# A decoder layer on one core: one gate pair moved from plain products in attention to the seven-product form

## The chip, the cores and the metric

The kernel runs on one core of a Trainium2 chip. The metric is the time of one execution in device microseconds; a time given for a kernel is the median of several runs. A profiled execution, taken by the hardware profiler, gives the rows that are read below. Engines: PE is TensorE's matrix products (PEld its weight loads), DVE is VectorE, ACT is ScalarE, POOL is GpSimd, SP is SyncE, which issues most of the loads.

## What is computed

One layer of a decoder on 512 tokens of width 1024, in float32. The parts around the change, shortened:

```python
proj = h @ w_in[l]
q, k, v, p, g = jnp.split(proj, [ATTN_WIDTH, 2 * ATTN_WIDTH, 3 * ATTN_WIDTH, 3 * ATTN_WIDTH + POOL_WIDTH], axis=-1)
y_attn = moba_attention(q.reshape(hs), k.reshape(hs), v.reshape(hs), rel_bias) @ w_branch_attn[l]
y_pool = multiscale_pool(p, w_pool_group[l], pool_scale[l]) @ w_branch_pool[l]
gates = jax.nn.sigmoid(g.astype(jnp.float32)).astype(h.dtype).reshape(B, S, N_BRANCHES, D)
mixed = gates[:, :, 0] * y_attn + gates[:, :, 1] * y_pool
h = layer_norm(ALPHA * h + mixed @ w_out[l], ln1_g[l], ln1_b[l])
a, u = jnp.split(h @ w_ffn_in[l], 2, axis=-1)
a = causal_dwconv(a, conv_w[l], conv_b[l])
f = (jax.nn.gelu(a, approximate=False) * u) @ w_ffn_out[l]
h = layer_norm(ALPHA * h + f, ln2_g[l], ln2_b[l])
```

Attention has 8 heads of 64. The gates are 2 x 1024 columns of the input projection: 8 output tiles of 128 for the attention branch and 8 for the pooling branch. A tile f of the first and the tile f of the second make a gate pair.

## The kernel before

**Products.** Every float32 operand is split into hi and lo parts (`split`, L71 to L78: ACT copies hi, DVE subtracts to get lo). `mm3` (L241) makes a product of three: hi by hi (L243), hi weight by lo activation (L246), lo weight by hi activation (L247). A plain output tile (`in_tile`, L491) takes 8 row blocks x 3 products of 512 columns, 24 in all. A branch tile (`br_mm`, L640) has 4 row blocks: 12 products of 512.

**The seven-product form.** `seven` (L285) computes two output tiles at once as a 2 x 2 block product with seven block products in place of eight. The tokens are halved (t1, t2 of 256), the rows of the weights too. It needs four combinations of the activations, called nT1, T3, nT2, T4, formed once by `t_form` (L261; subtractions at L264 and L267) and split; and combinations of the two weight tiles: A is the first tile as loaded, X a sum that the DMA makes (a plain load on SP at L188, an accumulating one on POOL at L190), D half of the second tile, Y comes from A and X by two DVE additions (L207). Each of the seven takes 4 row blocks x 3 products of 256 columns.

**Order of the stages.** v, the pooling tiles and q, k come first. Then attention runs as a loop over heads h = 0 to 7 (L656), two heads ahead: `head(h + 2)` casts keys and queries (k, kl the low part of the keys, q) and copies k and kl to the other 64 partitions by DMA (L454); then one filler for PE; `scores(h + 2)` (products sc; DVE adds the bias from strip and takes maxima nm, ACT takes exponentials at L561, POOL normalises at L566); `pv` of a pair of heads (products ob, L634); `trans(h)` (transposes tr, L621, copied to PT). The fillers of heads 0 to 3 are four plain gate tiles (g0, g8, g1, g9, `fill`); those of heads 4 to 7 are pooling-branch tiles (`early_branch`, L649; names br0_1 to br3_1, the 1 for pooling).

After the loop oT, the attention output (copied at L636), is split into oT_hi and oT_lo, and `order` (L708) lists the other branch tiles: br4_1, br5_1, br6_1, then the attention-branch tiles br6_0, br0_0 to br5_0. Beside them the four forms of x for the gates are made from four quads, which POOL loads at L676 behind the last normalisation, followed by X of the first gate pair (gX). Then six gate pairs f = 2 to 7 follow in the seven-product form (products sag, scg, sbg), then the tile br7 of both branches, the output projection (wo), and the FFN.

**What sets the order.** Each engine works through its own queue in the order in which a scheduler has put the instructions; `issue_after` forbids some to be put earlier. A PE product whose input is late keeps everything behind it waiting.

Of the kernel before, what the change touches and what calls it, by code (L numbers as in the profile page):

```python
# [8 lines left out]
F32 = mybir.dt.float32  # L9
# [5 lines left out]
P = 128  # L15
S = 512
# [3 lines left out]
H = 8  # L20
# [18 lines left out]
RAW = 1  # L39
KH = NF // 2  # L40
TAIL = 8
GSEVEN = 2
BRANCH = (("z", 0), ("z", 1), ("z", 2), ("br", 6), ("o", 0), ("o", 1), ("o", 2), ("br", 7))
SEVEN = tuple(range(2, 19))
COVER = 4
# [7 lines left out]
def layer_kernel(ctx: ExitStack, tc: tile.TileContext, xT, x, w_v, w_c, rel_bias, invcnt, w_group,  # L53
# [18 lines left out]
    def split(hi, lo, src, copy=None):  # L72
        if copy:
            copy(hi, src)
        else:
            state["hi"] = nc.scalar.activation(hi, src, AF.Copy)  # L76
        state["lo"] = nc.vector.tensor_tensor(lo, src, hi.bitcast(F32), op=ALU.subtract)  # L77
        return state["lo"]  # L78
# [8 lines left out]
    def add(key, *tiles):  # L87
        at[key] = len(chunks)
        chunks.extend(tiles)

    def add_seven(key, *two):
        pair_of[key] = two
        for q in "AXDY":
            add((*key, q), (key, q))
# [4 lines left out]
    for p in range(pairs):  # L99
        add_seven(("i", 1 + p), w_c[first["q"] + p], w_c[first["k"] + p])  # L100
    fill = [("g", 8 * g + f) for f in range(GSEVEN) for g in range(2)]
    for n, j in fill:
        add((n, j), w_c[first[n] + j])
    for n, key in enumerate(BRANCH[:-1]):
        add(key, w_br[n])
    for f in range(GSEVEN, KT):
        add_seven(("g", f), w_c[first["g"] + f], w_c[first["g"] + KT + f])
# [208 lines left out]
    zT = keepp.enter_context(tc.tile_pool(name="keepz", bufs=1)).tile([P, 4, S], F32, name="zT")  # L316
# [120 lines left out]
    def head(h, *behind):  # L437
        p, e = divmod(h, 2)
        own, oth = slice(e * DH, (e + 1) * DH), slice((1 - e) * DH, (2 - e) * DH)
        qb, kb = raw_q[p], raw_k[p]  # L440
        Q1[h] = av.tile([P, S], F32R, tag="q1", name=f"q1_{h}")
        K1[h] = av.tile([P, S], F32R, tag="k1", name=f"k1_{h}")
        KL[h] = av.tile([P, S], F32R, tag="kl", name=f"kl_{h}")
        with ExitStack() as held:
            for ins in behind:
                held.enter_context(tc.issue_after(ins.ins))
            nc.scalar.activation(K1[h][own, :], kb[own, :], AF.Copy, scale=-1.0)
            nc.vector.scalar_tensor_tensor(KL[h][own, :], kb[own, :], -1.0, K1[h][own, :].bitcast(F32),
                                           op0=ALU.mult, op1=ALU.subtract)
            nc.scalar.activation(flip(Q1[h][own, :]), qb[own, :], AF.Copy, scale=DH ** -0.5)  # L450
            nc.vector.scalar_tensor_tensor(flip(Q1[h][oth, :]), qb[own, :], DH ** -0.5,
                                           flip(Q1[h][own, :]).bitcast(F32), op0=ALU.mult, op1=ALU.subtract)
        for t in (K1[h], KL[h]):
            state["dup"] = nc.sync.dma_start(t[oth, :].bitcast(F32), t[own, :].bitcast(F32))  # L454
# [36 lines left out]
    def in_tile(kind, j):  # L491
        wh, wl = split3(weights(at[kind, j]), KT)
        b = bank(f"{kind}{j}")
        for kt in range(KT):
            mm3(b, (wh[:, kt, :], wl[:, kt, :]), (xT_hi[:, kt, :], xT_lo[:, kt, :]), kt == 0, kt == KT - 1)
        if kind == "p":
            return b
        else:
            gslot[j] = gates[:, len(gslot), :]
            nc.scalar.activation(gslot[j], b, AF.Copy)  # L500
# [39 lines left out]
    def scores(h):  # L540
        if h + 2 < H:
            load_strip(h + 2)
        pp = aw.tile([P, 10 * P], F32, tag="pp", name=f"pp{h}")
        nm = aw.tile([P, NT], F32, tag="nm", name=f"nm{h}")
        rs = aw.tile([P, NT], F32, tag="rs", name=f"rs{h}")
        b01 = bank(f"sc{h}_01")
        dst = [b01[:, :2 * P], b01[:, 2 * P:], bank(f"sc{h}_2")[:, :3 * P], bank(f"sc{h}_3")]
        for i in range(NT):
            n = max(2, i + 1) * P
            q = slice(i * P, (i + 1) * P)  # L550
            nc.tensor.matmul(dst[i], Q1[h][:, q], K1[h][:, :n], start=True, stop=False)
            nc.tensor.matmul(dst[i], Q1[h][:, q], KL[h][:, :n], start=False, stop=True)
        for i in range(NT):
            n = (i + 1) * P
            nc.vector.tensor_tensor_reduce(out=pp[:, offs[i]:offs[i] + n], in0=dst[i][:, :n],
                                           in1=strips[h][:, S - n:], scale=1.0, scalar=-3.0e38,
                                           op0=ALU.add, op1=ALU.max, accum_out=nm[:, i:i + 1])
        nms[h] = nc.vector.tensor_scalar(nm, nm, -1.0, None, op0=ALU.mult)  # L558
        for i in range(NT):
            n = (i + 1) * P  # L560
            exps[h] = nc.scalar.activation(pp[:, offs[i]:offs[i] + n], pp[:, offs[i]:offs[i] + n], AF.Exp,  # L561
                                           bias=nm[:, i:i + 1], accum_out=rs[:, i:i + 1])
        nc.vector.reciprocal(rs, rs)  # L563
        for i in range(NT):
            n = (i + 1) * P
            state["norm"] = nc.gpsimd.tensor_scalar(pp[:, offs[i]:offs[i] + n], pp[:, offs[i]:offs[i] + n], rs[:, i:i + 1], 1.0,  # L566
                                    op0=ALU.mult, op1=ALU.mult)
        Ps[h] = pp
# [33 lines left out]
            scores(0)  # L602
    phase.close()
    keep = keepp.enter_context(tc.tile_pool(name="keep", bufs=1, reuse_waits="tile"))
    gates = keep.tile([P, 2 * GSEVEN + 4, S], F32, name="gates")
    oT = keep.tile([P, 4, S], F32, name="oT")
    zT_hi = keep.tile([P, 4, S], F32R, name="zT_hi")
    zT_lo = keep.tile([P, 4, S], F32R, name="zT_lo")
# [31 lines left out]
    def br_mm(f, br, b=None, ks=range(4), pin=False):  # L640
        key, o = (("br", f), 4 * br) if f >= 6 else (("oz"[br], f // 2), f % 2 * 4)
        wh, wl = split3(weights(at[key]), KT)
        b = b or bank(f"br{f}_{br}")
        for k in ks:
            src = (zT_hi[:, k, :], zT_lo[:, k, :]) if br else (oT_hi[:, k, :], oT_lo[:, k, :])
            mm3(b, (wh[:, o + k, :], wl[:, o + k, :]), src, k == 0, k == 3, pin and k == ks[0])
        return b

    def early_branch(f):  # L649
        t = branch[f, 1] = gates[:, 2 * GSEVEN + f, :]  # L650
        nc.vector.tensor_copy(t, br_mm(f, 1))
# [4 lines left out]
    for h in range(H):  # L656
        if h + 2 < H:
            head(h + 2, nms[h], exps[h])
        if h < 4:
            in_tile(*fill.pop(0))  # L660
        elif h < H - 1:
            early_branch(h - 4)
        if h + 2 < H:
            scores(h + 2)
        with ExitStack() as held:
            if h and h % 2 == 0:
                pv(h // 2 - 1)
                held.enter_context(tc.issue_after(state["pv"].ins))
            trans(h)
        if h < 4:  # L670
            with tc.issue_after(nms[h].ins), tc.issue_after(exps[h].ins):
                split(zT_hi[:, h, :], zT_lo[:, h, :], zT[:, h, :])
        if h == 5:
            with tc.issue_after(state["norm"].ins), tc.issue_after(state["dup"].ins):
                for n, (k, t) in enumerate(((k1, t1), (k1, t2), (k2, t1), (k2, t2))):
                    nc.gpsimd.dma_start(quads[n], xT[k.start * P:k.stop * P, t].rearrange("(k p) t -> p k t", p=P))  # L676
                homes["g", "X"], homes["g", "D"] = lambda f: gX, lambda f: gD
                for q in "XD":
                    coming[q].remove(("g", GSEVEN))
                    fetch_raw(("g", GSEVEN), q)  # L680
                    homes.pop(("g", q))
        if h == H - 1:
            early_branch(h - 4)
    pv(H // 2 - 1)
    attn.close()

# [4 lines left out]
    more = bp.tile([P, 4, S], F32, name="more")  # L691
# [11 lines left out]
        nc.gpsimd.tensor_tensor(a, b, a, op=ALU.add)  # L703
        mts[f] = a

    unused = [more[:, n, :] for n in range(4)]
    forms = list(parts)
    order = [(4, 1), (5, 1), (6, 1), (6, 0)] + [(f, 0) for f in range(6)]  # L708
    for n, (f, br) in enumerate(order):
        if f < GSEVEN:  # L710
            with tc.issue_after(state["o"].ins):
# [35 lines left out]
    for f in range(GSEVEN, KT):  # L747
        if f == KT - 1:
# [3 lines left out]
              lambda ba, u, f=f: gate_done(f, ba, u), first_half if f == KT - 1 else None)  # L752
# [434 lines left out]
```

## Time and profile before

| | before |
|---|---|
| median of 3 runs | 627.27 us (626.81 to 627.68) |
| the profiled execution | 627.02 us, span 625.3 us |
| mean granted TensorE clock | 0.995 |
| PE busy | 615.4 us (98%) |
| DVE busy | 514.8 us (82%) |
| ACT busy | 361.6 us (58%) |
| POOL busy | 119.4 us (19%) |

Busy time of PE counts products that overlap as one stretch; the time that a product adds is the distance from its start to the next start. In the rows a timeline line gives start and duration, both in us from the span's start, then engine, line, operation, output and inputs, and in brackets the idle time before it with what ended that.

### The profile page before, as it was taken

What the parts mean: (1) busy time and instruction counts of PE and PEld (TensorE: products, weight loads), DVE (VectorE), ACT (ScalarE), POOL (GpSimd) and SP (SyncE); (2) the same over time, 40 slices, a digit from 0 to 9 for tenths busy, and PEclk for the clock granted to TensorE, in tenths of its full rate; (3) what the DMA queues carried; (4) which work ended last, traced back from release to release, by engine and by line L of the source; (5) the groups of instructions that cost most, each with busy time, mean ns of one, the idle gap of its engine ahead of it and who ended that gap; (6) DMA issues with size and microseconds to landing.
All of it is one profiled execution on the core that took longest, in us unless ns stands there. A gap on an engine that the chain in (4) does not pass through costs nothing.

```text
span 625.3 us, 10604 instructions
## 1 busy us (share of the span) xinstructions
PE 615.4 (98%) x4060; PEld 554.7 (89%) x4060; DVE 514.8 (82%) x790; ACT 361.6 (58%) x552; POOL 119.4 (19%) x133
## 2 busy tenths in 40 slices
PE   8999999999999999999999999999999999999994
PEld 6899998786799998889999999999999888888884
DVE  5978788784967988399989988898988859698886
ACT  5746778663756567125566566566656356555442
POOL 0133135244032101110110101101100302123302
PEclk9999999999999999999999999999999999999998
DMA  8566747435386414806658777678635996899805
GB/s 313 168 191 192 172 122 226 123 118 185 118 206 181 102 67 171 301 36 210 161 167 215 181 197 186 180 195 206 184 96 163 329 248 134 211 194 207 197 0 135
DMA packets 41634, 109.29 MB, mean 175 GB/s; under 512 B 4448, under 2 KB 4712, under 8 KB 41328
## 3 DMA queue, kind: packets, MB, share of 16 engines
q1 hardware_dynamic: 27808, 72.42, 33.9%
q0 software_dynamic: 13200, 35.15, 29.2%
q10 hardware_dynamic: 576, 1.05, 0.5%
q8 instruction: 32, 0.52, 0.3%
q14 instruction: 18, 0.15, 0.1%
HBM read 104.39 MB, written 3.17 MB: 172 GB/s over the span
## 4 chain that ended last, share of the span: by engine, by line
PE 97%; DVE 1%; DMA 1%; ACT 0%; POOL 0%; issue 0%; DVEq 0%; POOLq 0%; ACTq 0%
PE saf L243 5%; PE saf L247 5%; PE saf L246 5%; PE v L426 3%; PE fi L243 3%; PE fi L246 3%; PE fi L247 3%; PE sbf L243 3%; PE sbf L246 3%; PE sbf L247 3%; PE wo L247 2%; PE wo L246 2%; PE wo L243 2%; PE br L243 2%; PE br L247 2%; PE br L246 2%
## 5 line engine op out<-in xcount | busy, mean ns | idle before, releaser
L77 DVE TENSOR_TENSOR wlo<-araw,whi 128x1024 fp32r<-128x1024 f32 x56 | 68.2, 1225 | 7.2 <-ACT whi L76 6.7
L76 ACT ACTIVATE whi<-araw 128x1024 fp32r<-128x1024 f32 x56 | 58.6, 1058 | 25.5 <-PE saf L246 5.6
L76 ACT ACTIVATE whi<-wraw 128x1024 fp32r<-128x1024 f32 (+1 forms) x49 | 49.7, 1020 | 34.2 <-DMA wraw<-in_w_fo 8.4
L77 DVE TENSOR_TENSOR wlo<-wraw,whi 128x1024 fp32r<-128x1024 f32 (+1 forms) x49 | 58.4, 1197 | 12.2 <-ACT whi L76 11.9
L76 ACT ACTIVATE whi<-tw 128x1024 fp32r<-128x1024 f32 (+1 forms) x30 | 29.5, 984 | 25.1 <-DMA tw<-in_w_fo 10.4
L190 POOL DMA_DIRECT2D xraw<-in_w_fi x15 | 18.1, 1206 | 134.3 <-DMA xraw<-in_w_fi 74.3
L77 DVE TENSOR_TENSOR wlo<-tw,whi 128x1024 fp32r<-128x1024 f32 (+1 forms) x30 | 33.4, 1129 | 8.6 <-ACT whi L76 8.6
L243 PE MATMUL saf<-hT_hi,whi 128*128 128x256 f32 x136 | 37.9, 279 | 0.0
L243 PE MATMUL sbf<-T_hi,whi 128*128 128x256 f32 x136 | 37.9, 279 | 0.0
L243 PE MATMUL saf<-nT_hi,whi 128*128 128x256 f32 x136 | 37.8, 278 | 0.0
L246 PE MATMUL saf<-hT_lo,whi 128*128 128x256 f32 x136 | 37.8, 278 | 0.0
L247 PE MATMUL saf<-nT_hi,wlo 128*128 128x256 f32 x136 | 37.8, 278 | 0.0
L247 PE MATMUL sbf<-T_hi,wlo 128*128 128x256 f32 x136 | 37.7, 278 | 0.0
L246 PE MATMUL sbf<-T_lo,whi 128*128 128x256 f32 x136 | 37.7, 277 | 0.0
L246 PE MATMUL saf<-nT_lo,whi 128*128 128x256 f32 x136 | 37.7, 277 | 0.0
L247 PE MATMUL saf<-hT_hi,wlo 128*128 128x256 f32 x136 | 37.7, 278 | 0.0
L246 PE MATMUL fi<-hT_lo,whi 128*128 128x256 f32 (+1 forms) x112 | 36.2, 326 | 0.0
L247 PE MATMUL fi<-hT_hi,wlo 128*128 128x256 f32 (+1 forms) x112 | 36.2, 325 | 0.0
L243 PE MATMUL fi<-hT_hi,whi 128*128 128x256 f32 (+1 forms) x112 | 36.1, 327 | 0.0
L566 POOL TENSOR_SCALAR pp<-pp,rs 128x128 f32<-128x128 f32 (+3 forms) x32 | 23.8, 759 | 30.7 <-DVE rs L563 23.2
L231 POOL DMA_DIRECT2D tw<-in_w_fo x18 | 15.6, 900 | 62.8 <-DVE wlo L77 61.2
L561 ACT ACTIVATE pp<-pp,nm 128x128 f32<-128x128 f32 (+3 forms) x32 | 17.6, 551 | 13.9 <-DVE nm L558 13.9
(355 smaller groups left out, 2216.7 us busy)
## 6 DMA issues: line engine op xcount, KB each, us to landing
tw<-in_w_fo POOLq DMA_DIRECT2D x20, 512.0 KB, 7.9
araw<-in_w_fi SPq DMA_DIRECT2D x17, 512.0 KB, 3.5
xraw<-in_w_fi SPq DMA_DIRECT2D x15, 512.0 KB, 4.0
xraw<-in_w_fi POOLq DMA_DIRECT2D x15, 512.0 KB, 6.4
araw<-in_w_c SPq DMA_DIRECT2D x11, 512.0 KB, 4.3
wraw<-in_w_fi SPq DMA_DIRECT2D x10, 512.0 KB, 4.1
wraw<-in_w_fo SPq DMA_DIRECT2D x10, 512.0 KB, 4.8
tw<-in_w_fo SPq DMA_DIRECT2D x10, 512.0 KB, 6.6
```

Of the source, the lines that this page charges most:

```text
L76: state["hi"] = nc.scalar.activation(hi, src, AF.Copy)
L77: state["lo"] = nc.vector.tensor_tensor(lo, src, hi.bitcast(F32), op=ALU.subtract)
L190: state["acc"] = nc.gpsimd.dma_start(v, bass.AP(tensor=a.tensor, offset=a.offset, ap=[[pst, pn], [u.offset + S - a.offset, 2], [est, S]]), ...
L231: nc.gpsimd.dma_start(raw, half(then[1:], sl), accum_op=ALU.add)
L243: ins = nc.tensor.matmul(out_, wh, ah, start=start, stop=False, **kw)
L246: nc.tensor.matmul(out_, wh, al, start=False, stop=False, **kw)
L247: nc.tensor.matmul(out_, wl, ah, start=False, stop=stop, **kw)
L426: ins = nc.tensor.matmul(bs[j], xs_[j][a], (wh, wl)[b], start=kt == 0 and n == 0, stop=False)
L561: exps[h] = nc.scalar.activation(pp[:, offs[i]:offs[i] + n], pp[:, offs[i]:offs[i] + n], AF.Exp, bias=nm[:, i:i + 1], accum_out=rs[:, i:i ...
L566: state["norm"] = nc.gpsimd.tensor_scalar(pp[:, offs[i]:offs[i] + n], pp[:, offs[i]:offs[i] + n], rs[:, i:i + 1], 1.0, op0=ALU.mult, op1=A ...
```

## The change

The constant GSEVEN counts the gate pairs that are made as plain tiles; it goes from 2 to 1. Two gate tiles (g0, g8) stay in attention as fillers of heads 0 and 1. The fillers of heads 2 to 7 are the pooling-branch tiles br0_1 to br5_1. The splits of the pooling output zT are made two per head under heads 0 and 1, where it was one per head under heads 0 to 3. The list behind the loop loses br4_1 and br5_1. Seven gate pairs, f = 1 to 7, take the seven-product form. The tile of buffers `gates` keeps its 8 places; one result finds its place in zT.

```diff
-GSEVEN = 2
+GSEVEN = 1
...
-    gates = keep.tile([P, 2 * GSEVEN + 4, S], F32, name="gates")
+    gates = keep.tile([P, H, S], F32, name="gates")
...
-        if h < 4:
+        if fill:
             in_tile(*fill.pop(0))
         elif h < H - 1:
-            early_branch(h - 4)
+            early_branch(h - 2 * GSEVEN)
...
-        if h < 4:
+        if h < 2 * GSEVEN:
             with tc.issue_after(nms[h].ins), tc.issue_after(exps[h].ins):
-                split(zT_hi[:, h, :], zT_lo[:, h, :], zT[:, h, :])
+                for k in range(2 * h, 2 * h + 2):
+                    split(zT_hi[:, k, :], zT_lo[:, k, :], zT[:, k, :])
...
         if h == H - 1:
-            early_branch(h - 4)
+            early_branch(h - 2 * GSEVEN)
...
-    unused = [more[:, n, :] for n in range(4)]
+    unused = [more[:, n, :] for n in range(4)] + [zT[:, 1, :]]
     forms = list(parts)
-    order = [(4, 1), (5, 1), (6, 1), (6, 0)] + [(f, 0) for f in range(6)]
+    order = [(6, 1), (6, 0)] + [(f, 0) for f in range(6)]
```

On PE at the end of attention, where the last output (ob) is finished and the attention branch begins, the order before is this. It shows the end of ob and the first of nine remaining products of br6_1 (br_1_1832); the three rows on zT come twice more behind it:

```order
L634 MATMUL ob_1750<-PT_1719,vv 64x256
L634 MATMUL ob_1750<-PT_1702,vv 64x128
L634 MATMUL ob_1750<-PT_1719,vv 64x128
L243 MATMUL br_1_1832<-zT_hi,whi_1523 128x512
L246 MATMUL br_1_1832<-zT_lo,whi_1523 128x512
L247 MATMUL br_1_1832<-zT_hi,wlo_1524 128x512
```

In the same place the changed kernel has this (br_1_1765 is br6_1, whose last product stands here ahead of ob; br_0_1779 is br6_0, the next ones br0_0, br1_0 and so on, seven in all, before the first row on oT_lo):

```order
L247 MATMUL br_1_1765<-zT_hi,wlo_1338 128x512
L634 MATMUL ob_1720<-PT_1689,vv 64x512
L634 MATMUL ob_1720<-PT_1672,vv 64x384
L634 MATMUL ob_1720<-PT_1689,vv 64x384
L634 MATMUL ob_1720<-PT_1672,vv 64x256
L634 MATMUL ob_1720<-PT_1689,vv 64x256
L634 MATMUL ob_1720<-PT_1672,vv 64x128
L634 MATMUL ob_1720<-PT_1689,vv 64x128
L243 MATMUL br_0_1779<-oT_hi,whi_1337 128x512
L243 MATMUL br_0_1806<-oT_hi,whi_1493 128x512
```

The nine products of br6_1 that stood behind the last output now stand ahead of it, and the first product on oT_hi follows the output directly.

On DVE in the same stretch, the order before (two lo parts of oT in one row, L264 and L267 are the forms, L207 the additions that make Y):

```order
L264 TENSOR_TENSOR quad0_82<-quad0_82,quad1_83 128x1024
L264 TENSOR_TENSOR quad1_83<-quad3_85,quad1_83 128x1024
L267 SCALAR_TENSOR_TENSOR quad3_85<-quad0_82,quad3_85 128x1024
L77 TENSOR_TENSOR wlo37_1873<-araw2_1868,whi37_1872 128x1024
L267 SCALAR_TENSOR_TENSOR quad2_84<-quad3_85,quad2_84 128x1024
L207 TENSOR_TENSOR araw2_1868<-gX_86,araw2_1868 128x512
L77 TENSOR_TENSOR oT_lo_1767<-oT_1094,oT_hi_1766 128x512 x2
```

And in the changed kernel:

```order
L77 TENSOR_TENSOR wlo35_1803<-araw1_1798,whi35_1802 128x1024
L264 TENSOR_TENSOR quad0_82<-quad0_82,quad1_83 128x1024
L264 TENSOR_TENSOR quad1_83<-quad3_85,quad1_83 128x1024
L267 SCALAR_TENSOR_TENSOR quad3_85<-quad0_82,quad3_85 128x1024
L207 TENSOR_TENSOR araw1_1798<-gX_86,araw1_1798 128x512
L77 TENSOR_TENSOR oT_lo_1737<-oT_1094,oT_hi_1736 128x512
L267 SCALAR_TENSOR_TENSOR quad2_84<-quad3_85,quad2_84 128x1024
```

The first lo part of oT now stands ahead of the fourth form, and still behind three forms and the addition that reads gX; the split of the first pair's A moved ahead of the forms.

## Rows read from the trace of the kernel before

**Rows 1.** Busy time by stretch: whole span, hand-over, gate pairs; engine columns, clock, DMA share, GB/s.

```profile
0.00:625.30 625.30, 615.40 (x4060) 554.70 (x4060) 514.84 (x790) 361.62 (x552) 119.37 (x133) 1.00 0.64 175
...
152.50:181.00 28.50, 28.50 (x132) 22.79 (x130) 22.50 (x24) 17.83 (x27) 5.93 (x4) 1.00 0.64 161
...
181.00:236.40 55.40, 55.40 (x481) 55.40 (x480) 45.48 (x57) 32.85 (x51) 8.77 (x7) 1.00 0.49 138
```

**Rows 2.** Waits of PE, longest first: us in total, times, longest.

```profile
PE warm_ps L341 <- DVE warm L338: 1.2, 1, 1.2
```

**Rows 3.** Timeline of PE, third gate tile's first product and the score product behind it.

```profile
118.86 0.48 PE L243 MATMUL g<-xT_hi,whi 128*128 128x512 f32 x1
...
124.42 0.28 PE L551 MATMUL sc<-k,q 128*128 128x256 f32 x1
```

**Rows 4.** Timeline of PE, first product of the pairs, first of br7.

```profile
180.96 0.28 PE L243 MATMUL sag<-xT_hi,whi 128*128 128x256 f32 x1
...
236.44 0.40 PE L243 MATMUL br<-zT_hi,whi 128*128 128x512 f32 x1
```

**Rows 5.** Timeline of PE, heads 4 and 5 of the loop.

```profile
130.59 0.40 PE L552 MATMUL sc<-kl,q 128*128 128x512 f32 x1
...
133.23 1.31 PE L621 MATMUL tr<-ident,pp 128*128 128x128 f32 x10
...
134.30 0.48 PE L243 MATMUL br<-zT_hi,whi 128*128 128x512 f32 x1
...
139.42 0.48 PE L243 MATMUL br<-zT_hi,whi 128*128 128x512 f32 x1
```

**Rows 6.** Timeline, head 7: last scores, a weight split between maxima, normalisation.

```profile
137.89 0.68 PE L552 MATMUL sc<-kl,q 128*128 128x256 f32 x3
...
138.87 1.22 DVE L77 TENSOR_TENSOR wlo<-wraw,whi 128x1024 fp32r<-128x1024 f32 x1
...
144.95 2.05 POOL L566 TENSOR_SCALAR pp<-pp,rs 128x128 f32<-128x128 f32 x4 [6.24 <-DVE rs L563]
```

**Rows 7.** Timeline, head 6: first key cast on ACT, last query part on DVE.

```profile
123.65 0.62 ACT L447 ACTIVATE k<-quad 64x512 fp32r<-64x512 f32 x1
...
125.06 0.85 DVE L451 SCALAR_TENSOR_TENSOR q<-quad,q 64x512 fp32r<-64x512 f32 x1
```

**Rows 8.** Landing times of L454, L676, L190; POOL's issues behind head 7's normalisation.

```profile
DMA to landing us min/median/max: 2.2/2.2/4.8
...
DMA to landing us min/median/max: 4.1/5.7/7.0
...
DMA to landing us min/median/max: 6.5/7.5/9.9
...
146.94 3.04 POOL L676 DMA_DIRECT2D quad<-in_xT  x4
...
149.97 1.26 POOL L190 DMA_DIRECT2D gX<-in_w_c  x1
```

**Rows 9.** Timeline of PE, transposes of heads 6 and 7.

```profile
144.66 2.27 PE L621 MATMUL tr<-ident,pp 128*128 128x128 f32 x16
```

**Rows 10.** Timeline at the hand-over, PE and ACT.

```profile
159.75 0.50 PE L243 MATMUL br<-zT_hi,whi 128*128 128x512 f32 x1
...
159.86 0.60 ACT L636 ACTIVATE oT<-ob 128x512 f32<-128x512 f32 x1 [2.14 <-PE ob L634]
...
160.35 1.67 ACT L76 ACTIVATE oT_hi<-oT 128x512 fp32r<-128x512 f32 x3
```

**Rows 11.** Timeline of DVE at the hand-over: a form, the addition, two splits.

```profile
156.28 1.23 DVE L264 TENSOR_TENSOR quad<-quad,quad 128x1024 f32<-128x1024 f32 x1 [1.47 <-DMA quad<-in_xT]
...
160.95 0.68 DVE L207 TENSOR_TENSOR araw<-gX,araw 128x512 f32<-128x512 f32 x1
...
161.56 1.28 DVE L77 TENSOR_TENSOR oT_lo<-oT,oT_hi 128x512 fp32r<-128x512 f32 x2
```

**Rows 12.** Timeline of PE, the program's first products.

```profile
1.25 2.74 PE L341 MATMUL warm_ps<-warm 128*128 128x512 bf16 x6 [1.25 <-DVE warm L338]
```


## The prediction

> **What bounds the kernel now.** I read the busy times by stretch first: TensorE (PE) is busy for 615.40 of 625.30 us, VectorE (DVE) for 514.84, the rest less [rows 1]. Then the waits of PE: the longest in the whole program is 1.2 us, for its very first operand [rows 2]. So a microsecond saved elsewhere is worth nothing, one PE product less is worth its issue interval, and any new wait of PE is a loss in full. Busy times of pipelined products overlap, so I take intervals between starts. A plain gate tile is 24 products of 512 columns; its first starts at 118.86 and the score product behind it at 124.42: 5.56 us, 227 ns a product and about 0.09 us more where PE comes from transposes [rows 3]. Between the first product of the gate pairs and the first of the last branch tile stand 480 products of 256 columns in 55.48 us: 115.6 ns each [rows 4].
>
> **The change part by part, against the profiled execution's own 627.02 us** (0.25 below the median of the three runs, 627.27; 1.7 of it lies outside the span).
>
> *PE work.* Two gate tiles leave: 2 x 5.56 = 11.12 us. Two branch tiles step up behind transposes in their place and pay the 0.09 us there: 0.18 us back. A seventh pair comes: 7 products x 4 row blocks x 3 = 84 instructions x 115.6 ns = 9.71 us. Net -1.23 us, all on the path. It is not 1/8 of 11.12 (1.39), since two 256-column products cost 231 ns against 227 for one of 512.
>
> *Attention.* A head with a branch tile as filler takes PE 5.12 us (134.30 to 139.42), and every second one 2.41 more for an output (130.59 to 133.23, less 0.23 of the score product in front): 12.65 us per two heads [rows 5]. With gate tiles it was longer; the new program has the short form from the third head on. What must fit beside it is the loop from one head's scores to those of the head two later. Head 7's scores end near 138.4 and its normalisation begins at 144.95; without the split of a weight tile in between (1.22) its exponentials are thus done within about 5.3 us [rows 6]. Casting keys and queries takes from 123.65 to 125.91, 2.3 us [rows 7]; their copy to the other 64 partitions lands in 2.2 us as a rule [rows 8]; a set of scores is 1.3 us (5.12 less a branch tile of 2.8 and transposes of 1.07). Sum 11.1 us, under 12.65, so PE still leads. I charge 0.3 us for single late copies; ends 0 (the rule holds) and 2.6 (one copy takes the longest landing, 4.8, and PE waits for all of it). In the old program the transposes of heads 6 and 7, 16 in a row, took 2.27 us; ten of an earlier head took 1.31, and six more at their 0.107 (133.23 to 134.30, ten) make 1.95: 0.3 us of waiting for normalised rows [rows 5, 9]. There is more work ahead of them now: -0.3.
>
> *The hand-over behind attention, first wait.* In the old order nine products of branch tile 6 stand between the last attention output and the first product that reads oT_hi. They run from 159.75 on, and cover ScalarE's copy of the output (159.86) and the first split (160.35, three in 1.67, so the first is there at about 161.0) [rows 10]. In the new order that tile stands whole ahead of the output, the next PE row reads oT_hi, and ScalarE's queue keeps copy, then split. Nothing covers 159.75 to 161.0: +1.25 us. Ends 1.1 and 1.4; no reading of the order makes it zero.
>
> *The hand-over, second wait.* After seven hi products PE needs the lo half of the first block. On VectorE (DVE) it stands behind three of the four forms and behind the addition that reads gX. POOL issues the four quads and then gX's accumulation right behind the last head's normalisation: 3.04 us of issues, landings 4.1 to 7.0 us behind a quad's issue, 6.5 to 9.9 (median 7.5) behind gX's [rows 8]. Counted from the end of that normalisation: last quad 2.3 + 7.0 = 9.3, then two forms of 1.2, the addition and the split (about 0.6 each): 12.9 [rows 11]; by gX, 3.0 + 9.9 + 1.2 = 14.1 at worst. I take 13.3, since in the old trace a 512 KB weight load ran beside gX that now goes out earlier. From the end of head 7's scores to the end of its normalisation the old trace has 8.6 us (138.4 to 147.0), of which a weight split of 1.22 in DVE's queue now stands behind the maxima: about 7.4 [rows 6]. Sum 20.7 us. PE's own way there from the same scores: three sets of transposes 3.3, three branch tiles 3 x 2.8, two outputs 2.4 + 2.85 (one is cut in two), the first wait 1.25, seven products 1.6: 19.8 us [rows 3, 5]. So PE waits 0.9 us; ends 0 (the quads land in the 4.1 of the first) and 3.0 (8.6 + 14.1 - 19.8 is 2.9, and a little for semaphores). In the old order two more branch tiles stood here; they are spent inside attention now.
>
> *Hidden.* The forms, splits and the new pair's weights cost VectorE and ScalarE more, but in the stage of the pairs VectorE is busy for 45.48 of 55.40 us (7.9 per pair of 9.7), ScalarE for 32.85, the DMA engines for half [rows 1]. Loading the pair takes 1.75 MB against 1.0: free at that share. The stretch before it loses 5.4 us of PE time while its DVE work (22.50 of 28.50) stays almost whole [rows 1]; the first X product comes late in it, so I charge 0, ends 0 and 1.5; if that cover fails, the first pair is late and the later ones, with 1.8 us of room each, catch up. The four splits of zT now go out under two heads instead of four: DVE does 1.3 us more by head 1, which delays head 2's maxima and nothing that PE reads before head 4. Order and code behind the pairs stay.
>
> **Sum:** 627.02 - 1.23 - 0.3 + 1.25 + 0.9 + 0.3 = **627.9**, 0.1% over the median.
>
> **Rivals.** (1) *The saving arrives whole:* 627.02 - 1.23 - 0.3 = 625.5. For it speaks that PE had almost no wait in any stage so far; against it that ScalarE's copy and split are 1.1 us in a row with nothing of PE's left beside them. It would need other waits to go that rows 2 doesn't show.
> (2) *The landing of gX decides:* slower. Place: VectorE's queue behind the forms. Price: the second wait at its upper end, 3.0 in place of 0.9: 630.0. It decides (over 628.5) once the lo half comes 13.8 us or later behind the normalisation, or the chain from the scores to it stays at the old 8.6. For it: 9.9 is what gX took in this very place; against it: the load that ran beside it is gone.
> (3) *Attention becomes bound by its latency:* heads two apart follow each other more slowly than 12.65 us. Price: PE waits once for a late copy, 2.6 in place of 0.3: 630.2. For it: the new PE order sets the products with kl, the low keys, behind transposes, as if they came late; against it the loop of 11.1 us.
> (4) *The clock falls in the hand-over.* All stretches ran at the full level so far [rows 1]. The first products of the program ran at the lower of the two levels, 1.2 GHz: six of 512 columns in 2.74 us, over 0.4 each against 0.227 [rows 12]. If two waits of 1.25 and 0.9 us with little between brought the lower level back for a stretch as long as that one, nearly half of it is lost, 1.3 us: 629.2. Against it: no gap of PE in this trace is so long, so rows show neither.
> The Trainium skill, "TensorE: Matmul & The Clock Gate", section "Part 1: The HAM clock gate", says that the throttled clock is the default state and that idleness of TensorE brings it back. By that rule the two waits would cost more than their length and the time would be 629.2 rather than 627.9; the start of this trace agrees with a slow beginning, and nothing in it shows a fall in mid-program.
>
> **How the numbers follow.** Chances: the forecast 0.53, the whole saving 0.07, gX 0.25, latency 0.10, the clock 0.05. 0.2%, or 1.25 us, is about what a measurement of this kernel can tell from no change. The forecast with its small charges varied (626.7 without the last two, 628.3 with a second wait of 1.3) lies inside 0.2% of the median: same 0.53; faster 0.07; slower 0.25 + 0.10 + 0.05 = 0.40. The range leaves out rival 1 and the far ends of the slow ones: 626.6 to 629.9.
>
> **What would show it.** In the new profile: gate pairs with 564 products of 256 columns at 115 to 116 ns; a PE gap of about 1.25 us between the last ob product and the first br product on oT_hi, with ScalarE's oT and oT_hi inside it; a gap of 0 to 3 us before the first product on oT_lo, with VectorE waiting for gX or a quad; no PE wait over 0.5 us in heads 2 to 7; clock at 1.00 there. The prediction is wrong if the first gap is missing, if PE waits for q, k or kl by microseconds, or if the pairs wait for their splits. A time under 626 would say that I have missed a wait that the old order held; one over 630 that the hand-over costs more than its parts.

## The result and the profile after

The changed kernel takes **633.14 us** (median of 5 runs, 631.85 to 633.19) against 627.27 (5 runs, 626.81 to 627.94): ratio 1.0081, 95% interval 1.0069 to 1.0093. It is slower where 0.6 us was forecast: the medians lie 5.9 us apart, the ratio stands for 5.1. The time lies outside the range. One run of the last experiment, 686 us at a mean granted clock of 0.85, is left out of every number below. The profiled execution took 631.85 us, 4.83 over the profiled one of before.

By stretch (times, span, then busy us and instructions of PE, PEld, DVE, ACT, POOL, then clock, DMA share, GB/s), first the changed kernel, for [rows 1]:

```profile
0.00:630.10 630.10, 616.23 (x4096) 555.87 (x4096) 520.79 (x799) 362.92 (x554) 120.74 (x134) 0.99 0.64 175
...
111.50:114.20 2.70, 0.37 (x2) 0.00 (x0) 2.67 (x3) 2.68 (x10) 0.84 (x2) 0.97 0.57 140
114.20:118.00 3.80, 3.69 (x11) 1.62 (x13) 2.05 (x4) 1.06 (x2) 2.91 (x4) 0.57 0.66 209
153.50:157.00 3.50, 2.29 (x15) 1.42 (x12) 2.60 (x3) 1.42 (x3) 0.00 (x0) 1.00 0.80 146
```

and the second and third of these stretches in the kernel before:

```profile
111.50:114.20 2.70, 2.70 (x14) 2.23 (x13) 1.46 (x4) 1.15 (x5) 0.18 (x1) 1.00 0.48 94
114.20:118.00 3.80, 3.80 (x27) 2.19 (x26) 2.53 (x9) 3.75 (x8) 2.24 (x4) 1.00 0.53 181
```

Two things stand out in the middle of attention: TensorE (PE) is busy for 0.37 us of 2.70, and behind that pause the granted clock is 0.57 where the old kernel had 1.00. The waits of PE in the changed kernel name the first, and a second one that was forecast; [rows 2] had only the start:

```profile
PE sc L551 <- DMA k<-k: 2.4, 1, 2.4
...
PE br L243 <- ACT oT_hi L76: 1.2, 1, 1.2
```

PE at that place, changed kernel: the last product of the first branch tile, head 4's scores, the first output, and much later the 16 transposes of heads 6 and 7, for [rows 9].

```profile
111.48 0.39 PE L247 MATMUL br<-zT_hi,wlo 128*128 128x512 f32 x1
114.31 1.30 PE L551 MATMUL sc<-k,q 128*128 128x256 f32 x3 [2.44 <-DMA k<-k]
115.54 3.31 PE L634 MATMUL ob<-PT,vv 128*64 128x512 f32 x16
...
144.13 1.97 PE L621 MATMUL tr<-ident,pp 128*128 128x128 f32 x16
```

The same output in the kernel before takes 2.38 us, not 3.31:

```profile
115.49 2.38 PE L634 MATMUL ob<-PT,vv 128*64 128x512 f32 x16
```

**Why the keys are late.** VectorE (DVE), ScalarE and SP's queue ahead of head 4's key copy, changed kernel:

```profile
102.65 0.68 DVE L77 TENSOR_TENSOR zT_lo<-zT,zT_hi 128x512 fp32r<-128x512 f32 x1
103.25 1.21 DVE L77 TENSOR_TENSOR wlo<-wraw,whi 128x1024 fp32r<-128x1024 f32 x1
104.39 0.68 DVE L624 COPY PT<-tr 128x512 f32<-128x512 f32 x1
104.99 0.41 DVE L625 COPY PT<-tr 128x256 f32<-128x256 f32 x1
105.32 1.21 DVE L77 TENSOR_TENSOR wlo<-wraw,whi 128x1024 fp32r<-128x1024 f32 x1
106.45 0.15 DVE L558 TENSOR_SCALAR nm<-nm 128x4 f32<-128x4 f32 x1
...
108.85 0.62 ACT L447 ACTIVATE k<-quad 64x512 fp32r<-64x512 f32 x1
...
109.50 0.47 SPq L454 DMA_DIRECT2D k<-k  x1
```

and before:

```profile
103.45 0.15 DVE L558 TENSOR_SCALAR nm<-nm 128x4 f32<-128x4 f32 x1
103.52 0.41 DVE L625 COPY PT<-tr 128x256 f32<-128x256 f32 x1
103.86 1.21 DVE L77 TENSOR_TENSOR wlo<-wraw,whi 128x1024 fp32r<-128x1024 f32 x1
...
105.84 0.61 ACT L447 ACTIVATE k<-quad 64x512 fp32r<-64x512 f32 x1
...
106.48 0.47 SPq L454 DMA_DIRECT2D k<-k  x1
```

Two more splits of zT, and with them a copy of PT and a weight split, now stand ahead of head 2's negated maxima (L558). These come 3.0 us later, and so do the exponentials, the cast of head 4's keys behind them and the copy. PE, meanwhile, reaches head 4's scores 2.4 us earlier than before (111.7 for 114.1): its filler under head 2 is a branch tile, not a gate tile.

The copy itself is slow, in both kernels. By the last of its 16 semaphore updates in the trace it lands 4.3 us after its issue before (at 110.8) and 4.7 in the changed kernel (at 114.2), where 2.2 is usual. The view of landings leaves this copy out; it has the copy of the low keys right behind, before and then changed:

```profile
DMA to landing us min/median/max: 3.9/3.9/3.9
...
DMA to landing us min/median/max: 4.2/4.2/4.2
```

So the old kernel had 3.3 us of slack (110.8 to 114.1). Issue, landing and PE take 3.02 + 0.33 + 2.40 = 5.75 of it: 2.46 too much, and PE starts 0.14 behind the landing, which makes the wait of 2.60 between products (2.44 of it idle). With the usual 2.2 us the keys would have been there at 111.7, just as PE arrives; that is an estimate, no run here makes the copy faster.

**The hand-over**, changed kernel, for [rows 10, 11]:

```profile
153.18 2.37 PE L634 MATMUL ob<-PT,vv 128*64 128x512 f32 x14
...
155.58 0.60 ACT L636 ACTIVATE oT<-ob 128x512 f32<-128x512 f32 x1 [5.37 <-PE ob L634]
...
156.07 1.66 ACT L76 ACTIVATE oT_hi<-oT 128x512 fp32r<-128x512 f32 x3
...
156.75 1.90 PE L243 MATMUL br<-oT_hi,whi 128*128 128x512 f32 x7 [1.21 <-ACT oT_hi L76]
...
156.82 0.69 DVE L207 TENSOR_TENSOR araw<-gX,araw 128x512 f32<-128x512 f32 x1
157.43 0.68 DVE L77 TENSOR_TENSOR oT_lo<-oT,oT_hi 128x512 fp32r<-128x512 f32 x1
...
158.49 0.40 PE L246 MATMUL br<-oT_lo,whi 128*128 128x512 f32 x1
```

The first wait is there, with copy and split inside it; the second is not: the lo half is ready at 158.1, as the seven hi products end. Against [rows 4], the first product of the pairs behind the branch tiles and the first of br7 are

```profile
180.17 0.28 PE L243 MATMUL sag<-xT_hi,whi 128*128 128x256 f32 x1
...
241.18 0.40 PE L243 MATMUL br<-zT_hi,whi 128*128 128x512 f32 x1
```

Between them stand 528 products in 61.01 us: 115.6 ns each, as before. The other 36 of the forecast's 564 were done earlier, among the branch tiles. The seventh pair has its price and no more.

**The balance.** Take the stretch from the first gate product in attention to the first product with the output weights, and give each product the usual interval to the next of its size (227 ns for 512 columns, 178 for 384, 115.5 for 256, 109 for 128, medians of both traces). What an interval has beyond that is a wait, a low clock or a seam (a longer step from one group of products to another):

| us | before | changed |
|---|---|---|
| products at their usual intervals | 154.17 | 152.97 |
| beyond them, in all | 1.78 | 7.42 |
| of it: up to head 4's first score product | 0.1 | 2.7 |
| head 4's first scores and the output behind them | -0.1 | 1.4 |
| last output, up to the first product on oT_hi | 0.4 | 1.5 |
| all else | 1.4 | 1.7 |
| the stretch | 155.95 | 160.39 |

Work fell by 1.20; 2.6 of waiting, 1.5 of low clock, 1.1 of hand-over and 0.4 in small pieces came. Before the stretch the changed run is 0.3 us later, behind it the two traces take the same (372.36 and 372.37 us to the end of the last product). That is the 4.8 us between the spans.

### The profile page after: what moved, and what is told of

Read it like the earlier page. It is cut to its first block, busy times and chain, and to the rows that moved or that the text cites. A ratio compares the mean times of both kernels' runs of the same rounds, so it can differ in the third digit from the quotient of the medians.

```text
span 630.1 us, 10697 instructions
## 1 busy us (share of the span) xinstructions
PE 616.2 (98%) x4096; PEld 555.9 (88%) x4096; DVE 520.8 (83%) x799; ACT 362.9 (58%) x554; POOL 120.7 (19%) x134
## 4 chain that ended last, share of the span: by engine, by line
PE 95%; DVE 2%; DMA 1%; ACT 1%; issue 0%; DVEq 0%; ACTq 0%
PE saf L243 5%; PE saf L247 5%; PE saf L246 5%; PE v L426 3%; PE fi L243 3%; PE fi L246 3%; PE fi L247 3%; PE sbf L243 3%; PE sbf L247 2%; PE sbf L246 2%; PE wo L246 2%; PE wo L243 2%; PE wo L247 2%; PE br L243 2%; PE sag L247 2%; PE sag L243 2%
## 5 line engine op out<-in xcount | busy, mean ns | idle before, releaser
L77 DVE TENSOR_TENSOR wlo<-araw,whi 128x1024 fp32r<-128x1024 f32 x58 | 71.0, 1232 | 7.1 <-ACT whi L76 6.5
L76 ACT ACTIVATE whi<-araw 128x1024 fp32r<-128x1024 f32 x58 | 60.8, 1060 | 25.0 <-PE saf L246 5.4
L77 DVE TENSOR_TENSOR wlo<-wraw,whi 128x1024 fp32r<-128x1024 f32 (+1 forms) x47 | 56.1, 1201 | 12.6 <-ACT whi L76 12.3
L76 ACT ACTIVATE whi<-wraw 128x1024 fp32r<-128x1024 f32 (+1 forms) x47 | 47.6, 1019 | 30.3 <-DMA wraw<-in_w_fo 8.7
L190 POOL DMA_DIRECT2D xraw<-in_w_fi x15 | 18.1, 1204 | 134.6 <-DMA xraw<-in_w_fi 57.2
L246 PEld LDWEIGHTS saf<-hT_lo,whi 128*128 128x128 f32 x136 | 25.5, 188 | 0.0
```

The costliest lines, as they stand in the source:

```text
L190: state["acc"] = nc.gpsimd.dma_start(v, bass.AP(tensor=a.tensor, offset=a.offset, ap=[[pst, pn], [u.offset + S - a.offset, 2], [est, S]]), ...
L246: nc.tensor.matmul(out_, wh, al, start=False, stop=False, **kw)
```

## The experiments

Unless said otherwise each is an edit of the changed kernel; times of before are those taken beside it.

**Head 4's keys.** The two extra splits under head 1 put behind head 2's negated maxima:

```diff
-                for k in range(2 * h, 2 * h + 2):
-                    split(zT_hi[:, k, :], zT_lo[:, k, :], zT[:, k, :])
+                with tc.issue_after(nms[2 * h].ins):
+                    for k in range(2 * h, 2 * h + 2):
+                        split(zT_hi[:, k, :], zT_lo[:, k, :], zT[:, k, :])
```

> The changed kernel with one edit: the splits of the two extra pooled tiles under head 1 are put behind head 2's maxima negation on VectorE, so that 1.36 us of work leaves the chain that leads to head 4's key copies. Theory A (the loss is TensorE's wait of 2.6 us for head 4's key copy, the low clock of 3.4 us that follows it and costs about 2.4 us more, and 1.25 us in the hand-over): the key copies are issued near 106.5 us again, the wait before head 4's scores is under 0.5 us, no stretch has a granted clock below 0.9, and the time is 633.1 - 2.6 - 2.4 = 628.1 us (626.9 to 628.4, ratio to before 0.999 to 1.002). Rival B (the copies are late because they land slowly beside the strip's and the weights' transfers, 4.2 us instead of 2.2, whenever they are issued): the wait shrinks by less than 1.5 us, the clock still falls, and the time is 631 to 632.5 us. Rival C (the loss sits in the pairs of the gates or the hand-over, and the wait in attention is made up for later): 633 us, unchanged.

Measured: 630.23 us (8 runs, 629.12 to 632.56), ratio 1.0044 [1.0028, 1.006]. Wait and low clock are gone, so what B and C expected does not come; but 2.1 us are missing from what A promised; 0.9 of them is A's own, who put the low clock at 2.4 where the balance has 1.5. B's premise does hold: the copy is issued at 107.06 and still takes 4.6 us, to 111.7, just ahead of PE. Waits of PE, PE round head 4 and at head 6, and the stretch that had the low clock:

```profile
PE br L243 <- ACT oT_hi L76: 1.2, 1, 1.2
PE saf L243 <- ACT fT L297: 1.1, 1, 1.1
```

```profile
111.83 0.77 PE L551 MATMUL sc<-k,q 128*128 128x256 f32 x3
112.53 1.72 PE L634 MATMUL ob<-PT,vv 128*64 128x512 f32 x6
114.18 0.39 PE L552 MATMUL sc<-kl,q 128*128 128x256 f32 x1
...
126.22 0.80 PE L551 MATMUL sc<-k,q 128*128 128x256 f32 x3 [0.45 <-DVE q L451]
```

```profile
113.00:116.00 3.00, 3.00 (x18) 1.62 (x15) 1.14 (x7) 2.98 (x10) 0.69 (x2) 1.00 0.50 175
```

Up to the output weights the intervals are 5.36 us beyond the usual ones, 2.1 less than the changed kernel's 7.42, although wait and low clock made up 4.1. Head 4's scores are now cut in two round the output (1.2 us of seams, worked out as above), head 7's transposes take 0.6 more, and head 6's wait for q adds 0.3. (The wait in saf, far behind, stands in no other profile here; this execution took 631.67 us, 1.4 over the median.) My reading is that an earlier PE comes closer to the heads' chain on the other engines; no run tests that by itself.

**The late copy without the short cover.** Kernel before, with the splits as the change has them:

```diff
-        if h < 4:
+        if h < 2:
             with tc.issue_after(nms[h].ins), tc.issue_after(exps[h].ins):
-                split(zT_hi[:, h, :], zT_lo[:, h, :], zT[:, h, :])
+                for k in range(2 * h, 2 * h + 2):
+                    split(zT_hi[:, k, :], zT_lo[:, k, :], zT[:, k, :])
```

> The kernel before with one part of the change: the four splits of the pooled tiles go two and two behind heads 0 and 1, and its four gate tiles stay in attention. VectorE's order round head 2 is then that of the changed kernel, and head 4's key copies are issued about 2.5 to 3 us later than before, but a gate tile of 5.56 us stands ahead of head 4's scores where the change has a branch tile of 3.0. Theory A (the wait needs both, the late copy and the shorter cover): a wait of at most 0.6 us and no fall of the clock, 627.3 to 627.9 us, within 0.1% of before. Rival (the late copy alone holds TensorE, by 2 us or more, and drops the clock): 629.5 to 632 us.

Measured: 627.82 us (11 runs) against 627.32 (16 runs), ratio 1.0008 [0.9999, 1.0017].

```profile
106.79 0.16 DVE L558 TENSOR_SCALAR nm<-nm 128x4 f32<-128x4 f32 x1
...
109.82 0.47 SPq L454 DMA_DIRECT2D k<-k  x1
...
114.54 0.39 PE L247 MATMUL g<-xT_hi,wlo 128*128 128x512 f32 x1
114.77 0.69 PE L551 MATMUL sc<-k,q 128*128 128x256 f32 x3
```

```profile
114.20:118.00 3.80, 3.80 (x21) 1.90 (x19) 3.26 (x5) 2.90 (x6) 3.18 (x4) 1.00 0.60 196
```

The negation and the copy are as late as in the changed kernel (the copy lands at 114.4, 4.6 us after its issue), the gate tile covers them, head 4's scores follow it without a wait, and the clock stays at 1.00. The loss needs both halves: a chain 3.0 us later and a PE that comes 2.4 us sooner. The slow landing was there throughout: 4.3 to 5.0 us for this copy in all fourteen traces.

**The hand-over.** The first branch tile divided round the last output:

```diff
-        b = br_mm(f, br)
+        if n == 0:
+            b = br_mm(f, br, None, range(2))
+            with tc.issue_after(state["pv"].ins):
+                b = br_mm(f, br, b, range(2, 4))
+        else:
+            b = br_mm(f, br)
```

> The changed kernel with one edit: the first branch tile after attention is computed half before and half behind the last head pair's output, so that TensorE has six products to do while ScalarE copies that output and splits its first part. Theory A: the 1.2 us wait for the first split attention output goes, nothing takes its place since the next gate operand (gX) had landed by then, and the time is 633.1 - 1.2 = 631.9 us; head 4's wait and the low clock behind it stay as they are. Rival D (what ends the hand-over is the gate operand's landing or VectorE's split, which the first wait only hides): the wait moves to the second part and the time stays at 633.1 us.

Measured: 631.42 us (5 runs), ratio 1.0055 [1.004, 1.007]; 1.7 below the changed kernel's median, 1.3 below that of its second series (632.73, further down). The wait on oT_hi has left PE's waits, head 4's is still there:

```profile
PE sc L551 <- DMA k<-k: 2.7, 1, 2.7
```

So the first wait costs its length. Both edits together:

> Both edits together (the weight split of the sixth branch's tile is also put behind head 2's negation, which the first edit brings about by itself). Theory A: 628.1 - 1.2 = 626.9 us at most, 625.5 us where the clock's whole price goes as well; ratio to before 0.997 to 0.9995, so that the change comes out ahead of the kernel before by up to the 1.5 us that it saves TensorE. Rival B: 630 to 631.5. Rival C or D: 633.

Measured: 629.94 us (10 runs), ratio 1.0031 [1.002, 1.0041]: slower than before, and 3.0 us above the most that A allowed (626.9). With PE earlier, the second wait of the forecast appears, for the split that stands behind a form which waits for a quad:

```profile
156.94 0.50 PE L249 MATMUL br<-oT_lo,whi 128*128 128x512 f32 x1 [0.80 <-DVE oT_lo L77]
```

Next, the changed kernel again, and with the addition that reads gX put behind the first lo half:

> The changed kernel itself, on the chip and beside the runs of the three kernels that follow, with a second profile of it. Theory A (its time is 627.0 - 1.2 of work + 2.6 for head 4's key copy + about 1.4 to 2.4 of low clock + 1.25 in the hand-over, and in most runs about 1 us more, because the gate operand gX lands later than the 8.64 us after its issue that the first profile shows, and VectorE's split of the attention output is queued behind the addition that reads gX): 632.3 to 633.3 us, and if this profile shows gX landing 9.3 us or more after its issue, then also a wait of TensorE for that split, of 0.5 to 1.3 us. Rival (the spread of 1.3 us among its runs comes from elsewhere, the length of the low clock say): no such wait whatever the landing, and the low stretch longer than 3.4 us.

```diff
+                if key == ("g", GSEVEN):
+                    held.enter_context(tc.issue_after(state["oT_lo"].ins))
...
+        state.setdefault("oT_lo", state["lo"])
```

> The changed kernel with one edit: VectorE's addition that reads gX is put behind the split of the first part of the attention output, so that no split of it waits for gX. Theory A: the time is that of a run in which gX lands early, 631.9 us (631.5 to 632.3), about 1.2 under the changed kernel's median on this chip. Rival (TensorE is not held by that split, or the pairs' operands behind the addition are then late): unchanged, or up to 0.5 us slower.

Measured: 632.73 us (5 runs, 632.33 to 632.99) and 631.98 (5 runs, 631.73 to 633.16), beside a before of 627.32. In the second profile of the changed kernel gX landed 9.04 us after its issue (8.64 in the first) and 0.1 us stood before the first lo product; the edit's median is 0.75 lower, its runs overlap with the others. The direction is A's, but five runs each show neither it nor the amount. Head 4's wait and the low clock repeat: 2.5 us, and 1.48 us beyond the usual intervals in that output alone.

The same idea in the kernel with both edits, where a form and the addition go behind two lo halves:

```diff
-            with tc.issue_after(state["PT"].ins):
+            with tc.issue_after(state["PT" if len(forms) == len(parts) else "oT_lo"].ins):
                 t_form(forms.pop(0), tg, *quads)
...
```

> The two edits of the earlier run e3 (pooled splits behind head 2's negation, first branch tile divided round the last head pair's output) and, new, VectorE's second gate form and its addition put behind the first two splits of the attention output. Theory A: the 0.8 us wait for the split that showed in e3 goes and the time is 629.1 us (628.6 to 629.5) against 629.9. If the form that is now 1.3 us later holds the gate pairs, 629.9 or more. The change ahead of the kernel before (under 627.3) would contradict the account of small waits left in attention (about 1.5 us in e3's profile).

Measured: 629.0 us (6 runs), ratio 1.0032 [1.002, 1.0043], as A said. Its waits of PE behind the first operand's, the best version's:

```profile
PE ob L636 <- ACT PT L625: 0.4, 1, 0.4
PE sc L553 <- DVE q L453: 0.4, 1, 0.4
```

No wait over 0.4 us there, the clock at 1.00, and still 1.7 us behind the kernel before: 4.48 us beyond the usual intervals against 1.78, more than the 1.20 that was saved.

**The price of the clock.** Eleven products of no use in the pause:

```diff
+        if h == 4:
+            for _ in range(11):
+                nc.tensor.matmul(b01, Q1[3][:, :P], K1[3], start=True, stop=True)
```

> The changed kernel with eleven products of no use (one 128-row weight block by 512 columns, into the bank that head 4's scores overwrite), which TensorE does in the gap before head 4's scores. Theory A with the clock as its own term: head 4's scores start where they did (near 114.3 us), since the key copy lands no sooner, but no stretch has a low granted clock, and the time is 633.1 - 2.4 = 630.7 us (629.4 to 631). If the low clock has another cause than the gap, or costs nothing because the products behind it wait for data anyway: 633 us; if eleven products are more than the gap holds: later by what they exceed it, up to 0.5 us.

Measured: 632.9 us (4 runs), ratio 1.008 [1.0064, 1.0095]. The clock holds (the stretch that had 0.57):

```profile
114.00:118.00 4.00, 4.00 (x22) 1.92 (x22) 2.31 (x9) 0.61 (x2) 2.91 (x4) 1.00 0.64 201
```

and nothing is won: the transposes of heads 6 and 7 stand 1.3 us beyond their intervals, and in the new order head 5's negation comes behind a weight split. With that split (of one weight block) put behind it, by the hold of the diff further down:

> The earlier run e4 (eleven products of no use in the gap before head 4's scores) lost 1.3 us in front of head 7's transposes, because the order had moved a weight split of 1.2 us ahead of head 5's maxima negation on VectorE; here that split is put behind the negation, and the eleven products stay. Theory A (the low clock behind the gap stretches the products in it by about 1.65 us, and that is paid): no low clock, head 7's transposes wait 0.6 us at most, and the time is 632.8 - 1.65 = 631.1 us (630.6 to 631.6). Rival (what the low clock costs is hidden, since the heads' chain on VectorE, ScalarE and GpSimd sets when head 7's transposes can start, whatever TensorE does before): 632.5 to 633 us, with the saved time back as a wait somewhere before the end of attention.

Measured: 633.6 us (4 runs), ratio 1.0104, above what either theory expected; the transposes still stand 1.0 us beyond, and head 7's own negation now stood behind a weight split. So a pair of kernels that hold all splits under heads 4 to 6 behind the next head's negation, without and with the eleven products:

```diff
+                if state.get("hold"):
+                    held.enter_context(tc.issue_after(state["hold"].ins))
                 split(hi[:, sl], lo[:, sl], raw[:, sl])
...
+            state["hold"] = nms[h + 1] if h >= 4 else None
             early_branch(h - 2 * GSEVEN)
+            state["hold"] = None
```

> The changed kernel with VectorE's and ScalarE's splits of the weights that are fetched under heads 4 to 6 put behind the maxima negation of the head after (so that head 5's and head 7's negation never stands behind a weight split). It is the partner of the next run. Both theories: head 4's wait and the low clock as in the changed kernel, 632.7 us (632.0 to 633.2).

> The kernel of the run before plus the eleven products of no use in the gap before head 4's scores, so that the two differ in these products and in what they do to the clock, with the weight splits behind the negations in both. Theory A (the low clock stretches the products behind the gap by about 1.65 us, and that is paid): 1.65 us under its partner, 631.1 us (630.6 to 631.6). Rival (hidden: VectorE, ScalarE and GpSimd set the pace of the heads from there on): within 0.4 us of its partner.

Measured: 633.89 us (6 runs) and 632.53 (6 runs). The difference, 1.4, is near A's 1.65, but both are slower than A expected (632.0 to 633.2 and 630.6 to 631.6), and it is no clean price: the first has a wait of 1.1 us that the second has not,

```profile
PE sc L554 <- DVE q L454: 1.1, 1, 1.1
```

and the execution that was profiled is the slowest of its six (637.12 us), with the clock at its lower level from 115.9 to 122.8, twice as long as in the changed kernel (114.05 to 117.46):

```profile
118.00:122.00 4.00, 4.00 (x16) 1.43 (x12) 0.40 (x1) 0.00 (x0) 1.52 (x2) 0.50 0.30 66
```

The second is no better than the changed kernel's 632.73. So it stays open how much of the 1.5 us by which the low clock stretched the products the whole kernel pays: no version that kept the clock up got them back.

Last, e7 with the splits behind the negations:

> The three edits of e7 and the weight splits behind the negations. Theory A (what e7 has left over the kernel before, 1.7 us, is made of small waits in attention, of which 0.6 us stand before head 7's transposes): head 7's transposes wait 0.3 us less or not at all, 628.6 us (628.2 to 629.0), still 1 us over the kernel before. Rival (the pace of the heads is set by the chain and not by that wait): 629.0 us or more.

Measured: 629.3 us (11 runs), ratio 1.0033 [1.002, 1.0047]: what the transposes of heads 6 and 7 had beyond their intervals fell from 0.6 to 0.1 us, and the time is not better. The rival's time came; no version here beats the kernel before.

## Why the prediction was wrong

- *PE work, -1.23:* right; -1.20 in the trace, 115.6 ns a product.
- *Transposes, -0.3:* right; the 16 of heads 6 and 7 take 1.72 us to the next group (144.13 to 145.85), against 2.03 before.
- *First hand-over wait, +1.25:* right in place, cause and size (1.21 of idle time, 1.1 more than before in the balance; taking it away gave 1.3 to 1.7).
- *Second wait, +0.9:* too dear in the first profile (0), 0.1 in the second; it comes to 0.8 once PE is earlier (e3). Rival 2's gX landing does not decide.
- *Late copies, +0.3:* **the step that failed.** It was 2.6, the upper end: rival 3's price, at head 4. Two sentences led there. One set the loop of two heads (11.1 us) against PE's 12.65 and took it for settled; a loop says how fast heads follow each other, not where PE stands when the cover becomes shorter, once, under head 2. The loop was also fed with the usual landing of a key copy, 2.2 us, the median of a view that leaves out some copies. In the very trace that was read, the key copies of heads 3 and 4 took 4.9 and 4.3 us by their semaphore updates; in the changed kernel head 4's took 4.7, and by the estimate above that makes the difference between a wait and none. The other, in the paragraph on what is hidden, said of the splits that they delay "nothing that PE reads before head 4". Head 4 was where to go on: its keys hang on head 2's exponentials, its cover had just been cut by 2.4 us.
- *The clock:* at nothing in the sum, and as a rival placed in the hand-over with 0.05. There it stayed at 1.00 through 1.2 us of idle time; in attention it fell behind 2.4 us of it, and the products behind took 1.5 us longer. TensorE had been dense until then, and with products in the pause (e4) the clock held. The trace agrees with the rule cited from the Trainium skill, "TensorE: Matmul & The Clock Gate", section "Part 1: The HAM clock gate", that idleness brings the lower level back: 114.2 to 118.0 at 0.57, an output at 3.31 us for 2.38.

By the forecast's own terms: 627.0 - 1.2 - 0.3 + 1.1 + 2.6 + 1.5 = 630.7, and 0.3 for the later start, 0.3 more in front of head 6's scores and 0.2 behind the first product on oT_hi make 631.5, against 631.85 profiled. The other runs, about 1 us higher, have no trace but one (632.73: 0.5 more beyond the intervals in this stretch).

## What to carry to other kernels

A filler on the busiest engine is also the cover of a chain on the others. When a shorter one takes its place, follow the first consumer behind it back to what it hangs on, and add what the change puts into that chain: here 3.0 us and 2.4 us (the first brings no wait alone, as e8 shows; the second alone, in e1, costs seams) made 2.6 of wait, a low clock and an order full of seams. For a transfer in that chain take its own landing, not the usual one of its kind. Mending the waits one by one gave back about 4 of the 5.9 us and not the lead; that the rest is lost because the cover itself is gone is argued here, not shown.

## What was unexpected of the hardware

- A pause of TensorE in the middle of dense work, 2.44 us of idle time, brought the granted clock down, 0.57 in the mean of the 3.8 us behind it; in all five profiles with this pause (2.44 to 2.71 idle) it fell, and the hand-over's 1.2 us never brought it down.
- Head 4's query part on VectorE took 2.03 us where [rows 7] has 0.85, while GpSimd normalised head 2:

```profile
109.97 2.37 POOL L566 TENSOR_SCALAR pp<-pp,rs 128x128 f32<-128x128 f32 x4
...
110.84 2.03 DVE L451 SCALAR_TENSOR_TENSOR q<-quad,q 64x512 fp32r<-64x512 f32 x1
```

It ended before the key landed and held nobody here. GpSimd alone does not explain it: in the kernel before the same instruction also ran beside the normalisation of head 2 (106.25 to 109.18) and took 0.85. The 2.03 came back in all nine profiles in which this chain is late, e8 among them; the cause is open.
